# Loading expert weights two experts at a time, with a shorter program around it, in a mixture-of-experts kernel

## The chip, the cores and the metric

The kernel runs on one core of a Trainium2 chip. The metric is the device time of one execution in microseconds (us). Four runs of the kernel before took 181.02 to 181.21 us, with a median of 181.1 us. The profile of the kernel before is one more execution, of 181.01 us.

The engines by the names that the profile uses: PE is TensorE (matrix products), PEld its weight loads, DVE is VectorE, ACT is ScalarE, POOL is GpSimd, SP is SyncE. A trailing q (SPq, PEq) means the engine's sequencer. DMA transfers are issued by SP and POOL here and carried out by 16 DMA engines.

## What is computed

```python
def setup_inputs():
    n_experts, capacity, hidden, expert_hidden = 8, 256, 512, 2048
    # x (8, 256, 512), w1 (8, 512, 2048), w2 (8, 2048, 512), all float32

def reference(x, w1, w2):
    h = np.matmul(x, w1)
    h = np.maximum(h, 0)
    return np.matmul(h, w2).astype(np.float32)
```

Each of eight experts has its own two-layer network and its own 256 rows. The weights are 8.39 MB for one expert in fp32, 67.1 MB in all; x and the output are 4.19 MB each.

## The kernel before

All inputs come from HBM as fp32 and are used as bf16. POOL's DMAs convert while they load; the part of x that SP loads (`x_head`) arrives as fp32 and is converted by DVE.

**Storage.** `w1_sb` and `w2_sb` have `NS` = 4 slots each, and expert e uses slot e mod 4. x has no place of its own: it waits in slot 2 of `w2_sb` (`x_sb`) until it has been transposed into `xT`. `hT` holds one expert's hidden values, and `out_sb` the whole output in fp32.

**The order of work on each engine** is written out by hand inside one critical section (`tc.tile_critical`, line 101), with semaphores between the engines. Each engine enters it after SP has given a signal (SP's no-op of line 101).

- SP issues `x_head` (line 105), then waits for one weight load after another, in the order of `loads`, and tells PE of each through the counters `c_w1` and `c_w2` (lines 109 and 111). At the end it stores the last expert (line 113).
- POOL issues the rest of x (line 119), makes the identity matrix with an affine select (line 122; DVE has set the tile to zero before), and then issues all weight loads (line 154): w1 and w2 of experts 0 to 6, then w1 of expert 7 and its w2 in two halves, 17 loads. Before a load into a slot that was used, it waits until PE is through with the old content: the first layer of expert e - 4 for w1, the second layer for w2. The w2 load of expert 2 waits for the transposes, since x lies in that slot. Before the last half of w2, a tiny store of 3 KB is issued (line 146), and after it the store of experts 0 to 6 (line 157), which waits for expert 6's results and for the tiny store to land.
- PE transposes x (64 matmuls), and then does for each expert: take one count of `c_w1`; the first layer in two halves of 32 matmuls each; the second layer, 32 matmuls, taking a count of `c_w2` ahead of each half. All matmuls stand in the profile under the helper's line 243, and are told apart by what they write: `xt_ps`, `h_ps` (first layer), `o_ps` (second layer). Addresses are kept in registers; `set_expert` works out the next expert's, with the slot from a mod and a multiplication.
- ACT copies half of the transposed x, applies the Relu to the first layer's results (`h_ps` to `hT`, line 202), copies the last piece of the output (line 208), and waits for the two stores to land (lines 209 and 210).
- DVE clears the identity tile (line 172), converts `x_head` (line 176), copies the other half of the transposed x, and copies `o_ps` to `out_sb` (line 185).

Of the kernel before, what the change touches and what calls it, by code (L numbers as in the profile page):

```python
# [8 lines left out]
FP32 = mybir.dt.float32  # L9
BF16 = mybir.dt.bfloat16  # L10
PE = mybir.EngineType.PE

FIRST_FREE = 16512


@with_exitstack
def kernel(
# [7 lines left out]
    nc = tc.nc  # L25
    P = 128
# [30 lines left out]
    def allot(name, shape, dtype):  # L57
        nonlocal free
        places[name] = free
        t = nc.alloc_sbuf_tensor_at(name, shape, dtype, offset=free)  # L60
        free += math.prod(shape[1:]) * mybir.dt.size(dtype)
        return t
# [3 lines left out]
    xT = allot("xT", [P, K1, MC, E * P], BF16)  # L66
    hT = allot("hT", [P, K2, C], BF16)
    out_sb = allot("out_sb", [P, E, MC, H], FP32)
    x_head = allot("x_head", [P, HEAD * H], FP32)
    identity = allot("identity", [P, P], BF16)  # L70
    W1_AT, W2_AT, XT_AT = places["w1_sb"], places["w2_sb"], places["xT"]

# [7 lines left out]
    def sem(name):  # L80
        return tc.alloc_semaphore(name)


    d_head, d_x = sem("d_head"), sem("d_x")
    d_first, d_out, d_last = sem("d_first"), sem("d_out"), sem("d_last")

    s_zero, s_ident, s_cast = sem("s_zero"), sem("s_ident"), sem("s_cast")
    p_xt, p_h, p_o = sem("p_xt"), sem("p_h"), sem("p_o")
    v_out, v_last = sem("v_out"), sem("v_last")

# [1 line left out]
    c_h, c_o, c_w1, c_w2 = sem("c_h"), sem("c_o"), sem("c_w1"), sem("c_w2")  # L92


    loads = []
    for e in range(E - 1):
        loads += [(1, e, 0, 2), (2, e, 0, 2)]
    loads += [(1, E - 1, 0, 2), (2, E - 1, 0, 1), (2, E - 1, 1, 1)]
    d_w = [sem(f"d_w{i}") for i in range(len(loads))]

    with tc.tile_critical(no_gpsimd_drain=True):  # L101


        sp = nc.sync
        sp.dma_start(x_head[:], x_v[:, :HEAD * H]).then_inc(d_head, 16)
        for i, (w, e, h, n) in enumerate(loads):
            sp.wait_ge(d_w[i], 16)
            if w == 1:
                sp.sem_inc(c_w1, 1)
            else:  # L110
                sp.sem_inc(c_w2, n)
        sp.wait_ge(v_last, MC)
        sp.dma_start(
            out_v[:, E - 1, :], out_sb[:, E - 1].rearrange("p m h -> p (m h)")
# [1 line left out]


        pool = nc.gpsimd
        pool.dma_start(x_sb[:, HEAD * H:], x_v[:, HEAD * H:]).then_inc(d_x, 16)  # L119
        pool.wait_ge(s_zero, 1)  # L120

        pool.affine_select(  # L122
            out=identity[:],
# [4 lines left out]
            pattern=[[-1, P]],  # L128
            channel_multiplier=1,
        ).then_inc(s_ident)  # L130
        for i, (w, e, h, n) in enumerate(loads):


            old = e - NS
            if (w, e) == (2, 2):
                pool.wait_ge(p_xt, K1 * MC)
            if old >= 0 and h == 0:
                if w == 1:
                    pool.wait_ge(p_h, NG * (old + 1))
                else:  # L140
                    pool.wait_ge(p_o, MC * (old + 1))
            if i == len(loads) - 1:


                pool.wait_ge(v_out, 1)
                pool.dma_start(  # L146
                    out_v[:16, 0:5:2, :16], out_sb[:16, 0:5:2, 0, :16]
                ).then_inc(d_first, 16)
            if w == 2:
                src = w2_v[:, e, h:h + n, :].rearrange("p h n -> p (h n)")  # L150
                dst = w2_sb[:, e % NS, h * JH * H:(h + n) * JH * H]
            else:
                src, dst = w1_v[:, e, :], w1_sb[:, e % NS, :]
            pool.dma_start(dst, src).then_inc(d_w[i], 16)  # L154
        pool.wait_ge(v_out, 2)
        pool.wait_ge(d_first, 16)
        pool.dma_start(  # L157
            out_v[:, :E - 1, :], out_sb[:, :E - 1].rearrange("p e m h -> p e (m h)")
        ).then_inc(d_out, 16)
        pool.drain()  # L160

# [5 lines left out]


        dve = nc.vector
        dve.memset(identity[:], 0.0).then_inc(s_zero)  # L172
        dve.sem_inc(c_xt[0], 1)
        dve.sem_inc(c_o, MC)
        dve.wait_ge(d_head, 16)
        dve.tensor_copy(x_sb[:, :HEAD * H], x_head[:]).then_inc(s_cast)  # L176
        for ko in range(K1):
            dve.wait_ge(p_xt, ko * MC + 1)
            copy_xt(dve.tensor_copy, ko, 0).then_inc(c_xt[0])
# [10 lines left out]

        act = nc.scalar
        act.sem_inc(c_xt[1], 1)
        act.sem_inc(c_h, UG)
        for ko in range(K1):
            act.wait_ge(p_xt, ko * MC + 2)
            copy_xt(act.copy, ko, 1).then_inc(c_xt[1])
# [9 lines left out]
                ).then_inc(c_h)  # L206
        act.wait_ge(p_o, E * MC)
        act.copy(out_sb[:, E - 1, 1, :], o_ps[1][:]).then_inc(v_last)  # L208
        act.wait_ge(d_out, 16)
        act.wait_ge(d_last, 16)  # L210

# [31 lines left out]
        def loop(name, counter, times, body):  # L245
# [6 lines left out]

        reg = {
            n: pe.alloc_register(n)
            for n in ["count", "half", "slot", "x", "b1", "b2"]
            + [f"xt{ko}" for ko in range(K1)]
            + [f"a{i}" for i in range(12)]
        }
# [2 lines left out]
        def last_column(step):  # L261

            return (P - 1) * step * 2

        count = reg["count"]

        n = MC * (R // MC)

        def transposes():
            i = 0  # L270
            for m in range(MC):
                take(c_xt[m], 1)
                for r2 in range(R // MC):
                    if i % 6 == 0:
                        for k in range(i, min(i + 6, n)):
                            row = (k % (R // MC)) * MC + k // (R // MC)
                            pe.reg_add(bank[i // 6 % 2][k - i], reg["x"], row * H * 2)
                        if i + 6 > n:
                            pe.reg_add(reg["x"], reg["x"], 2)
                            pe.reg_add(count, count, 1)  # L280
                    t = matmul(
                        xt_ps[m][:, r2, :],
                        at(w2_sb, bank[i // 6 % 2][i % 6], [[K1, P]]),
                        pe.lower_ap(identity[:]),
                        start_tensor_calc=True,
                        stop_tensor_calc=True,
                        is_transpose=True,
                    )
                    i += 1
                t.then_inc(p_xt)  # L290

        pe.wait_ge(s_ident, 1)
        pe.wait_ge(s_cast, 1)
        pe.wait_ge(d_x, 16)
        pe.reg_mov(count, 0)
        pe.reg_mov(reg["x"], X_AT + last_column(K1))
        loop("transposes", count, K1, transposes)
        for m in range(MC):
            pe.wait_ge(c_xt[m], 1)

# [30 lines left out]
        def first_addresses():  # L331
            a, b, regs = CHUNKS1[0]
            compute(address1, range(a, b), regs)

        def set_expert():
            slot = reg["slot"]
            pe.reg_mod(slot, count, NS)
            pe.reg_mul(slot, slot, K1 * F * 2)
            pe.reg_add(reg["b1"], slot, W1_AT + last_column(K2))
            pe.reg_add(reg["b2"], slot, W2_AT)  # L340
            for ko in range(K1):
                pe.reg_add(reg[f"xt{ko}"], reg[f"xt{ko}"], P * 2)
            first_addresses()

        def half():
            n = JH * K1
            for i in range(n):
                j, ko = divmod(i, K1)
                c, r = place(CHUNKS1, i)
                if i == CHUNKS1[c][1] - 2:  # L350
                    if c + 1 < len(CHUNKS1):
                        next_chunk(CHUNKS1, c, address1)
                        if c + 2 == len(CHUNKS1):
                            pe.reg_add(reg["half"], reg["half"], 1)
                    else:
                        pe.reg_add(reg["b1"], reg["b1"], JH * 2)
                        first_addresses()
                        a, b, regs = CHUNKS2[0]
                        compute(address2, range(a, b), regs)
                g = j // GJ  # L360
                ends = j % GJ == GJ - 1 and ko == K1 - 1
                if ends:


                    take(c_h, 1)
                    if i == n - 1:
                        take(c_o, MC // 2)
                mm = matmul(
                    h_ps[g][:, (j % GJ) * C:(j % GJ + 1) * C],
                    at(w1_sb, r, [[K2, P]]),  # L370
                    at(xT, reg[f"xt{ko}"], [[E * P, MC], [1, P]]),
                    start_tensor_calc=ko == 0,
                    stop_tensor_calc=ko == K1 - 1,
                )
                if ends:
                    mm.then_inc(p_h)

        def expert():
            take(c_w1, 1)
            loop("half", reg["half"], 2, half)  # L380
            for k in range(K2):
                if k % JH == 0:
                    take(c_w2, 1)
# [4 lines left out]
                if k == CHUNKS2[c][1] - 1 and c + 1 < len(CHUNKS2):  # L388
                    next_chunk(CHUNKS2, c, address2)
                if k == CHUNKS2[-1][0] - 1:  # L390
                    pe.reg_add(count, count, 1)
                    pe.reg_add(reg["half"], reg["half"], -2)
                if k == K2 - 1:
                    set_expert()
                for m in range(MC):
# [7 lines left out]
                    if k == K2 - 1:  # L403
                        mm.then_inc(p_o)

        pe.reg_mov(count, 0)
        pe.reg_add(reg["half"], count, 0)
        pe.reg_add(reg["b1"], count, W1_AT + last_column(K2))
        pe.reg_add(reg["b2"], count, W2_AT)
        for ko in range(K1):  # L410
            pe.reg_add(reg[f"xt{ko}"], count, XT_AT + ko * MC * E * P * 2)
        first_addresses()
        take(c_h, 1)
        loop("expert", count, E, expert)


# [28 lines left out]
```

## Time and profile before

| What | Value |
|---|---|
| Median of four runs | 181.1 us |
| Profiled execution | 181.01 us |
| Its span, first to last instruction | 179.2 us |
| PE busy in the span | 131.0 us |
| ACT busy in the span | 38.7 us |
| Read from HBM, written to HBM | 71.30 MB, 4.20 MB |
| Mean of both over the span | 421 GB/s |
| Start of the first weight load's issue on POOL | 2.45 us |
| Landing of the first weight load (SP's line 109) | 22.6 us |
| Landing of the last weight load (SP's line 111) | 167.9 us |
| First matmul of the first layer | 25.18 us |
| Last store issued on SP (line 113) | 174.80 us |
| Landing of that store, after its issue | 3.1 us |
| Landing of the large store (line 157), after its issue at 163.85 us | 12.8 us |

How to read it: the span counts from the first instruction of the program to the last. The difference between the execution's time and the span, 1.8 us, lies outside what the profile shows of the program. A line of the timeline gives start, duration, engine, source line, operation, output and inputs, the number of instructions merged, and in brackets the idle time of the engine before it and what ended that. A line of the waits gives who waited for whom, the total, how often, and the longest. The page's slices cut the span into 40 equal parts and give a busy share in tenths; in the row PEclk it is the granted TensorE clock.

### The profile page before, as it was taken

Reading aid. Unit: us, or ns where it says so; the run is one execution under the profiler, and the core shown is the slowest. Engines: PE = TensorE matmul, PEld = TensorE weight load, DVE = VectorE, ACT = ScalarE, POOL = GpSimd, SP = SyncE. Lnnn points to the kernel's source line nnn. Section 1 sums busy time; section 2 is a strip of 40 time slices with the busy share of each in tenths; the row PEclk is TensorE's granted clock in tenths of the full one; section 3 lists DMA queues with packets and bytes.
Section 4 is the critical chain, followed back from the end, with each engine's and each line's share of the span. In section 5 each row is a group of like instructions: output and inputs, shape, how many; then the busy total and the mean of one; then the engine's idle time right before and its main releaser. Section 6 shows DMA issues by size and latency. Waiting matters only on the chain. (4 is left out here: it accounts for less than half of the span.)

```text
span 179.2 us, 2111 instructions
## 1 busy us (share of the span) xinstructions
PE 131.0 (73%) x832; PEld 91.6 (51%) x832; DVE 15.9 (9%) x21; ACT 38.7 (22%) x38; POOL 11.7 (7%) x25
## 2 busy tenths in 40 slices
PE   0008659998949494949987698949494998769980
PEld 0007548846924393417933595439341893359530
DVE  0204320002000200020002000020002000200010
ACT  2002423601520044001520044004400152004310
POOL 7100030101010101010011000020000000002000
PEclk9999999999999999996999889999999699978996
DMA  5999999998998999999899899999989989999995
GB/s 194 260 197 227 234 197 212 234 227 183 234 234 186 223 234 197 212 234 227 186 230 234 186 223 234 201 208 234 227 183 234 234 183 227 234 188 222 334 422 239
DMA packets 3824, 40.37 MB, mean 225 GB/s; under 512 B 368, under 2 KB 368, under 8 KB 1392
## 3 DMA queue, kind: packets, MB, share of 16 engines
q0 software_dynamic: 3536, 38.80, 97.1%
q1 hardware_dynamic: 288, 1.57, 2.4%
HBM read 71.30 MB, written 4.20 MB: 421 GB/s over the span
## 5 line engine op out<-in xcount | busy, mean ns | idle before, releaser
L243 PE MATMUL h_ps<-xT,w_sb 128*128 x512 | 67.1, 297 | 18.3 <-PEq L218 18.3
L243 PEld LDWEIGHTS h_ps<-xT,w_sb 128*128 x512 | 60.6, 148 | 26.6 <-issue 22.7
L243 PE MATMUL o_ps<-w_sb,hT 128*128 x256 | 56.5, 379 | 9.2 <-PEq L218 9.2
L202 ACT ACTIVATE hT<-h_ps 128x1024 bf16<-128x1024 f32 x32 | 32.7, 1023 | 111.2 <-PE h_ps L243 111.2
L243 PEld LDWEIGHTS o_ps<-w_sb,hT 128*128 128x128 bf16 x256 | 24.5, 98 | 39.0 <-issue 10.4
L185 DVE COPY out_sb<-o_ps 128x512 f32<-128x512 f32 x15 | 9.7, 686 | 141.2 <-PE o_ps L243 141.2
L243 PE MATMUL xt_ps<-identity,w_sb 128*128 128x128 bf16 x64 | 7.6, 311 | 15.7 <-PEq L218 15.7
L243 PEld LDWEIGHTS xt_ps<-identity,w_sb 128*128 x64 | 6.5, 146 | 16.5 <-issue 16.5
L154 POOL DMA_DIRECT2D w_sb<-in_w_dram x17 | 9.1, 540 | 87.5 <-PE h_ps L243 37.7
L165 ACT COPY xT<-xt_ps 128x1024 bf16<-128x1024 bf16 x4 | 4.0, 1012 | 18.0 <-PE xt_ps L243 18.0
L165 DVE COPY xT<-xt_ps 128x1024 bf16<-128x1024 bf16 x4 | 4.9, 1224 | 11.9 <-PE xt_ps L243 11.9
L157 POOL DMA_DIRECT2D out_dram<-out_sb x1 | 0.9, 947 | 44.3 <-DMA out_dram<-out_sb 44.3
L208 ACT COPY out_sb<-o_ps 128x512 f32<-128x512 f32 x1 | 0.6, 585 | 5.9 <-PE o_ps L243 5.9
L146 POOL DMA_DIRECT2D out_dram<-out_sb x1 | 0.6, 557 | 20.0 <-DVEq L188 20.0
L176 DVE CAST w_sb<-x_head 128x2048 bf16<-128x2048 f32 x1 | 1.2, 1226 | 4.5 <-DMA x_head<-in_x_dram 4.5
L165 ACT ACT_TABLE_LOAD x1 | 1.3, 1283 | 1.0 <-SPq L101 1.0
L119 POOL DMA_DIRECT2D w_sb<-in_x_dram x1 | 0.7, 679 | 1.0 <-DVE identity L172 1.0
L122 POOL TENSOR_SCALAR_AFFINE_SELECT identity<-identity 128x128 bf16<-128x128 bf16 x1 | 0.3, 304 | 0.1
L172 DVE MEMSET identity<- 128x64 uint32 x1 | 0.1, 112 | 1.0 <-SPq L101 1.0
L429 POOL MEMSET const-float32-0.0<- 128x1 f32 x1 | 0.1, 98 | 0.2 <-issue 0.2
L429 POOL MEMSET const-bfloat16-1.0<- 128x1 bf16 x1 | 0.1, 101 | 0.0
L429 POOL MEMSET const-uint8-127<- 128x1 uint8 x1 | 0.1, 101 | 0.0
(1 smaller groups left out, 0.1 us busy)
## 6 DMA issues: line engine op xcount, KB each, us to landing
w_sb<-in_w_dram POOLq DMA_DIRECT2D x15, 2048.0 KB, 65.3
out_dram<-out_sb POOLq DMA_DIRECT2D x1, 3584.0 KB, 12.8
w_sb<-in_w_dram POOLq DMA_DIRECT2D x2, 1024.0 KB, 57.0
w_sb<-in_x_dram POOLq DMA_DIRECT2D x1, 1536.0 KB, 11.4
x_head<-in_x_dram SPq DMA_DIRECT2D x1, 1024.0 KB, 4.7
out_dram<-out_sb SPq DMA_DIRECT2D x1, 512.0 KB, 3.1
out_dram<-out_sb POOLq DMA_DIRECT2D x1, 3.0 KB, 44.8
```

Of the source, the lines that this page charges most:

```text
L119: pool.dma_start(x_sb[:, HEAD * H:], x_v[:, HEAD * H:]).then_inc(d_x, 16)
L122: pool.affine_select(out=identity[:], in_=identity[:], compare_op=mybir.AluOpType.not_equal, fill=1.0, base=0, pattern=[[-1, P]], channel_ ...
L146: pool.dma_start(out_v[:16, 0:5:2, :16], out_sb[:16, 0:5:2, 0, :16]).then_inc(d_first, 16)
L154: pool.dma_start(dst, src).then_inc(d_w[i], 16)
L157: pool.dma_start(out_v[:, :E - 1, :], out_sb[:, :E - 1].rearrange("p e m h -> p e (m h)")).then_inc(d_out, 16)
L165: return copy(xT[:, ko, m].rearrange("k (ep r2) -> k ep r2", r2=R // MC), xt_ps[m][:].rearrange("k r2 ep -> k ep r2"),)
L176: dve.tensor_copy(x_sb[:, :HEAD * H], x_head[:]).then_inc(s_cast)
L185: cp = dve.tensor_copy(out_sb[:, e, m, :], o_ps[m][:])
L202: act.activation(hT[:, g * GJ:(g + 1) * GJ, :].rearrange("p a c -> p (a c)"), h_ps[g % UG][:], mybir.ActivationFunctionType.Relu,).then_in ...
L208: act.copy(out_sb[:, E - 1, 1, :], o_ps[1][:]).then_inc(v_last)
L243: return pe.add_instruction(inst)
L429: nc = _bacc.Bacc("TRN2", target_bir_lowering=False, num_devices=1)
```

## The change

The weight loads are regrouped. w1 of experts (0, 1), (2, 3) and (4, 5), and w2 of experts (0, 1) and (2, 3), are each loaded by one DMA into two neighbouring slots; the rest stays one load an expert, and the last w2 two halves. 17 loads become 12. A pair is announced to PE when both experts have landed. POOL's wait for free slots goes by the later expert of a pair.

With that come other edits:

- `x_head` is a tile of a pool now, and its load and conversion stand ahead of the critical section. All engines but POOL wait for the conversion when they enter it. POOL enters at once and waits for it just before the load of w2 for experts 2 and 3 (`tc.wait_critical_data_deps()`).
- POOL sets the identity tile to zero itself.
- Each slot has one semaphore for its landings, counted up, in place of one semaphore for each load; several others are merged into `d_pool` and `s_ident`.
- PE's expert loop has no counter of its own: the slot's address is stepped and wrapped (`next_slot`), the loop ends on the address of `xT`, and it jumps back to the head of the half loop. The count of `c_w1` is taken in each half, and SP adds two for each expert.
- POOL's drain and ACT's last waits stand behind PE's loop.
- The tiles' addresses move by 8,192 bytes per partition.

```diff
-FIRST_FREE = 16512
+FIRST_FREE = 16512 + 8192
...
     loads = []
-    for e in range(E - 1):
-        loads += [(1, e, 0, 2), (2, e, 0, 2)]
-    loads += [(1, E - 1, 0, 2), (2, E - 1, 0, 1), (2, E - 1, 1, 1)]
-    d_w = [sem(f"d_w{i}") for i in range(len(loads))]
+    for es in [(0, 1), (2, 3)]:
+        loads += [(1, es, 0, 2), (2, es, 0, 2)]
+    loads += [(1, (4, 5), 0, 2), (2, (4,), 0, 2), (2, (5,), 0, 2)]
+    for e in range(6, E - 1):
+        loads += [(1, (e,), 0, 2), (2, (e,), 0, 2)]
+    loads += [(1, (E - 1,), 0, 2), (2, (E - 1,), 0, 1), (2, (E - 1,), 1, 1)]
+    landed, counts = [], {}
+    for w, es, h, _ in loads:
+        s = d_half if h else (d_w1, d_w2)[w - 1][es[0] % NS]
+        counts[id(s)] = counts.get(id(s), 0) + 16
+        landed.append((s, counts[id(s)]))
+
+    x_pool = ctx.enter_context(tc.tile_pool(name="x_pool", bufs=1))
+    x_head = x_pool.tile([P, HEAD * H], FP32, tag="x_head")
+    nc.sync.dma_start(x_head[:], x_v[:, :HEAD * H])
+    nc.vector.tensor_copy(x_sb[:, :HEAD * H], x_head[:])
     with tc.tile_critical(no_gpsimd_drain=True):
 
         sp = nc.sync
-        sp.dma_start(x_head[:], x_v[:, :HEAD * H]).then_inc(d_head, 16)
-        for i, (w, e, h, n) in enumerate(loads):
-            sp.wait_ge(d_w[i], 16)
-            if w == 1:
-                sp.sem_inc(c_w1, 1)
-            else:
-                sp.sem_inc(c_w2, n)
+        for i, (w, es, h, n) in enumerate(loads):
+            sp.wait_ge(*landed[i])
+            sp.sem_inc((c_w1, c_w2)[w - 1], n * len(es))
...
-        pool.wait_ge(s_zero, 1)
+        pool.memset(identity[:], 0.0).then_inc(s_ident)
+        pool.wait_ge(s_ident, 1)
...
-            old = e - NS
-            if (w, e) == (2, 2):
+            old = es[-1] - NS
+            if w == 2 and 2 in es:
+                tc.wait_critical_data_deps()
                 pool.wait_ge(p_xt, K1 * MC)
...
+            e, ne, at_slot = es[0], len(es), es[0] % NS
             if w == 2:
-                src = w2_v[:, e, h:h + n, :].rearrange("p h n -> p (h n)")
-                dst = w2_sb[:, e % NS, h * JH * H:(h + n) * JH * H]
+                src = w2_v[:, e:e + ne, h:h + n, :].rearrange("p e h n -> p e (h n)")
+                dst = w2_sb[:, at_slot:at_slot + ne, h * JH * H:(h + n) * JH * H]
             else:
-                src, dst = w1_v[:, e, :], w1_sb[:, e % NS, :]
-            pool.dma_start(dst, src).then_inc(d_w[i], 16)
+                src, dst = w1_v[:, e:e + ne, :], w1_sb[:, at_slot:at_slot + ne, :]
+            pool.dma_start(dst, src).then_inc(landed[i][0], 16)
         pool.wait_ge(v_out, 2)
-        pool.wait_ge(d_first, 16)
+        pool.wait_ge(d_pool, 32)
...
-        act.wait_ge(d_out, 16)
-        act.wait_ge(d_last, 16)
...
+        def next_slot():
+
+            size, wrap = K1 * F * 2, reg["wrap"]
+            pe.reg_add(wrap, slot, -(NS - 2) * size)
+            pe.reg_alu(wrap, wrap, 0, mybir.AluOpType.max)
+            pe.reg_mul(wrap, wrap, NS)
+
         def set_expert():
-            slot = reg["slot"]
-            pe.reg_mod(slot, count, NS)
-            pe.reg_mul(slot, slot, K1 * F * 2)
+            pe.reg_add(slot, slot, K1 * F * 2)
+            pe.reg_sub(slot, slot, reg["wrap"])
...
         def half():
             n = JH * K1
+            take(c_w1, 1)
...
-        def expert():
-            take(c_w1, 1)
-            loop("half", reg["half"], 2, half)
+        def second_layer():
...
-        loop("expert", count, E, expert)
+        loop("half", reg["half"], 2, half)
+        second_layer()
+        pe.br_lt(reg["xt0"], xt_first[0] + E * P * 2, on_true="half_head", on_false="experts_end")
+        nc.switch_bb("experts_end")
+
+
+        pool.drain()
+        act.wait_ge(d_pool, 48)
+        act.wait_ge(d_last, 16).then_inc(s_ident)
```

## The prediction

> **What bounds the kernel now.** First the page: busy shares, the slices, the queues.
>
> ```profile
> span 179.2 us, 2111 instructions
> PE 131.0 (73%) x832; PEld 91.6 (51%) x832; DVE 15.9 (9%) x21; ACT 38.7 (22%) x38; POOL 11.7 (7%) x25
> PEclk9999999999999999996999889999999699978996
> DMA  5999999998998999999899899999989989999995
> q0 software_dynamic: 3536, 38.80, 97.1%
> ```
>
> TensorE is busy for 73% and the DMA engines are full in all slices but the first and last. Is the stream dense, or does it wait for anything? SP passes each landed weight load on, so its waits and the times of its two lines (109 for w1, 111 for w2) show the pace of the stream:
>
> ```profile
> SPq L109 <- DMA w_sb<-in_w_dram: 88.8, 8, 21.2
> SPq L111 <- DMA w_sb<-in_w_dram: 77.2, 9, 9.7
> ...
> L109 SPq EVENT_SEMAPHORE  x8: 17/17/17, 22.6 to 158.2; - x8
> ```
>
> (158.2 - 22.6) / 7 = 19.37 us an expert, for 8.39 MB of fp32 read: 433 GB/s. The landings of the trace are even: 22.58, 32.25, 41.95, 51.62 ... 148.49, 158.18, 163.04 and 167.93 us. No load was issued late: the median one was issued 65 us before it landed. Then the end, in the timeline:
>
> ```profile
> 155.55 1.29 DVE L185 COPY out_sb<-o_ps 128x512 f32<-128x512 f32 x2 [18.09 <-PE o_ps L243]
> 158.35 8.85 PE L243 MATMUL h_ps<-xT,w_sb 128*128 x64 [2.62 <-PEq L218]
> ...
> 163.85 0.95 POOL L157 DMA_DIRECT2D out_dram<-out_sb  x1 [44.30 <-DMA out_dram<-out_sb]
> ...
> 167.09 7.07 PE L243 MATMUL o_ps<-w_sb,hT 128*128 x32
> ...
> 174.19 0.58 ACT L208 COPY out_sb<-o_ps 128x512 f32<-128x512 f32 x1 [5.93 <-PE o_ps L243]
> 174.80 0.35 SPq L113 DMA_DIRECT2D out_dram<-out_sb  x1
> ```
>
> The page's chain (PE, then ACT) stops at the last computation, but the kernel does not: the store of experts 0 to 6 moves packets from 167.19 to 176.28 us, directly behind the last weights, and the last expert's store from 175.90 to 177.53. So the DMA engines have work without a pause from 1.96 us (first packet of x_head) to 177.53 us. Some 1.7 us of barriers follow. That is the bound: when the first byte moves, how densely the rest follows, and what is left behind the last one. TensorE waits 2.6 us before each expert.
>
> **The change part by part.**
>
> Start. SP's x_head load at line 105 starts at 0.95 us. Before it stand SP's signal to the critical section (line 101, at 0.73) and its wait for that signal (0.80). Afterwards the load stands ahead of both. It can gain nothing, or at most 0.95 - 0.73 = 0.22 us; I take 0.15, since its own setup stays. POOL no longer waits for SP's signal, so x's other load is issued no later; its packets started at 4.83 us only, when x_head's were nearly through. The price is that DVE, ACT, PE and SP now wait for the cast of x_head to enter the section, at about 6.9 us. Behind that wait stand ACT's table load (1.28 us; ACT's first copy is at 15.4), PE's transposes (they wait for x until 12.9 anyway) and SP's first landing (32 us). All covered. POOL's new memset, at most the 0.30 us of the affine select on the same tile, delays the first weight load from 2.45 us to about 3; x keeps the engines until 12.5. The no-op at line 149 holds POOL until the cast; the load behind it waits for the transposes (23.6 us) in any case.
>
> Five fewer loads. 17 become 12, with the same bytes. What does the boundary between loads cost? 2 MB take 9.686 us (148.493 to 158.179), a 1 MB half 4.865: 2 x 4.865 - 9.686 = 0.044 us per boundary. Five are worth 0.22 us if the cost is per load. The halves also have twice as many packets for their bytes, so it may lie in the packets, and then a pair gains nothing. The completion packet alone took 22 ns, half of the 44: I take 0.15. The other end: a pair's source has two rows per partition, 4 MB apart, which no row shows. Nearest is x's load, which takes 24 KB out of every 32 KB: 12,288-byte packets in 926 ns against 16,384 in 1,226 ns, so 26.5 against 26.7 B/ns read, 0.7% less. On 5 pairs x 19.37 us that loses 0.7 us.
>
> [...]
>
> When weights come. Without other shifts the pairs land at 32.25 (w1 of 0, 1), 51.62 (w2), 71.0 (w1 of 2, 3), 90.38 (w2), 109.74 (w1 of 4, 5); the rest as before. TensorE, with 7.38 us a first layer and 7.07 a second at full clock, and 1.7 more where it starts cold (the 3.4 us dips of the granted clock to 0.5 make 8.85 to 8.99 of 7.38): first layer of 0 at 32.4 to 41.3, wait; second layer at 51.8 to 60.6; expert 1 to 75.0; first layer of 2 to 82.4, wait 8 us; second at 90.5 to 99.3; then experts 3 to 6 without a wait, 4 x 14.45 = 57.8, to 157.1. Every load is there by then: w2 of 4 at 119.43 is wanted at 121, w2 of 5 at 129.11 wanted at 135, w2 of 6 at 148.49 wanted at 150. The delay is made good 1 us before w1 of 7 lands (158.18). The last expert then starts as now, and needs the last half of w2 (167.93) in any case.
>
> POOL's waits for free slots. w1 of (4, 5) now needs the first layer of expert 1 (75.0 - 7.07 = 67.9), with w2 of (2, 3) in the queue until 90.4; w2 of 4 and of 5 need 60.6 and 75.0; w1 of 6 needs 82.4; w2 of 6 needs 99.3, with work queued until 138.8; w1 and w2 of 7 need 106.7 and 113.7. The tiny store and the last half need expert 4's copies, about 128 + 1.6, and the half starts at 163. No gap; the least cover is 22 us, and beyond that delay each microsecond would lengthen the kernel by one.
>
> Tail. The big store still waits for the tiny one, which lands with the first half of w2. If TensorE is warm in the last expert it ends at 172.5 instead of 174.15, and the last store is issued 1.5 us earlier. But the engines are full: 1,024 output packets at 51 per 0.5 us take 10.04 us from 167.19, until 177.23 against 177.53. Gain 0 (cold) to 0.3; I take 0.1.
>
> Teardown. ACT takes one branch fewer behind the last wait (33 ns and its gap), and some 13 fewer semaphores stand in the range clear of 0.27 us: 0 to 0.2, I take 0.1. Register arithmetic on PE (no mod, three more operations) lies under matmuls until 90 us and then inside TensorE's 1 us of slack.
>
> Sum: -0.15 - 0.15 - 0.1 - 0.1 = -0.5 us. The profiled execution took 181.01 us, 179.2 of it span; 1.8 lies outside, unchanged. So 178.7 span and 180.5; its run stood 0.1 under the median of 181.1, so 180.6.
>
> **The rivals.**
>
> *Nothing arrives* (181.1): the boundary cost is in the packets, x_head's first bytes wait for something other than SP, and the tail is cold. For it: each term is a tenth or two, and none has a row of its own. Against: lines 101 and 105 stand in series.
>
> *The pairs read more slowly* (slower). Place: the five paired loads, 97 us of stream. Price: 0.7 us at x's pace, so 180.6 + 0.15 + 0.7 = 181.45; 1% is 1.0 us, 181.7. It outweighs the other gains (0.35) from 0.36% on. For it: the engines already run at 433 GB/s without slack, so any loss shows fully. Against: neither x's odd rows nor the change between w1 and w2 shows more than 0.7%.
>
> *TensorE becomes the bound* (slower). From 90.5 us it runs behind. With a cold start in each expert, 15.9 us instead of 14.45, it ends at 90.5 + 8.8 + 5 x 15.9 = 178.8, 4.6 late: 185. It decides from 15.0 us an expert (74.9 us left for five). The return from a second to a first layer is never seen without a DMA wait; the tightest, 41.45 to 42.12, allows at most 0.67 us, 15.1 an expert. Against: the dips follow idle stretches of 2.6 us, and there are none here.
>
> *More than I count* (180.0): the pairs' packets are larger, or fewer instructions shorten the 1.8 us outside the span.
>
> **How the numbers follow.** Forecast 0.54, nothing 0.22, slower reading 0.12, TensorE 0.06, more 0.06. The forecast's own range is 180.2 (all bounds: -0.22 - 0.22 - 0.3 - 0.2 = -0.94) to 181.0. The range of 180.0 to 181.6 takes in "nothing" and the near half of slower reading. The measurement tells 0.2%, 0.36 us, from no change. Faster, under 180.74: four fifths of the forecast and all of "more", 0.50. Same: a fifth of the forecast, "nothing", 0.32. Slower, over 181.46: 0.18.
>
> **What would show it.** Right: x_head issued near 0.8 us; paired landings 19.32 to 19.37 us apart; the last half landing near 167.6; PE without a wait from 90 to 156 us; last packet near 177.1. Wrong: paired landings over 19.5 us apart, a gap in the stream before w1 of 4 and 5, or the last expert's first layer starting after 159 us.

## The result: slower by a quarter of a per cent

The changed kernel takes 181.58 us (median of 46 runs, 181.27 to 182.49), the kernel before 181.13 us (70 runs beside it, 180.92 to 181.98). The ratio is 1.0025, with a 95% interval of 1.0019 to 1.0031. The profiled execution of the changed kernel took 181.40 us. The time lies inside the range that was given, but on the wrong side of no change: a gain of 0.5 us was forecast, and 0.45 us were lost.

The page of the changed kernel, with the rows that answer to those shown of before (the queues are the last three of them):

```profile
span 179.6 us, 2102 instructions
PE 128.0 (71%) x832; PEld 89.9 (50%) x832; DVE 15.8 (9%) x20; ACT 38.7 (22%) x38; POOL 10.3 (6%) x21
...
PEclk9999999999558999999558999999999999999998
DMA  6998999999899999999999999998999999899994
...
q0 software_dynamic: 3456, 38.80, 96.8%
q1 hardware_dynamic: 288, 1.57, 2.4%
q8 instruction: 1, 0.02, 0.0%
```

The page of before has two queues:

```profile
q0 software_dynamic: 3536, 38.80, 97.1%
q1 hardware_dynamic: 288, 1.57, 2.4%
```

The span is 0.4 us longer. POOL's queue (q0), which carries the weights, moves the same 38.80 MB in 3,456 packets, 80 fewer than before. The last row of the changed kernel is new: one transfer of instructions, 0.02 MB, on a queue of its own. It looks like nothing, at 0.0% of 16 engines' span. It turned out to be the difference between forecast and result. Below, "the transfer" means this one.

The start of `x_head` in the timeline of before, and then the start and the end in that of the changed kernel:

```profile
0.95 0.38 SPq L105 DMA_DIRECT2D x_head<-in_x_dram  x1
```

```profile
0.74 0.38 SPq L116 DMA_DIRECT2D x_head<-in_x_dram  x1
...
1.91 0.22 POOL L132 MEMSET identity<- 128x128 bf16 x1
...
2.81 2.18 POOL L169 DMA_DIRECT2D w_sb<-in_w_dram  x3 [0.15 <-issue]
...
74.42 7.51 PE L252 MATMUL h_ps<-xT,w_sb 128*128 x64
...
91.12 9.24 PE L252 MATMUL o_ps<-w_sb,hT 128*128 x31 [9.19 <-PEq L227]
...
158.92 7.49 PE L252 MATMUL h_ps<-xT,w_sb 128*128 x64 [1.32 <-PEq L227]
...
164.36 0.97 POOL L172 DMA_DIRECT2D out_dram<-out_sb  x1 [32.71 <-DMA out_dram<-out_sb]
...
166.31 7.07 PE L252 MATMUL o_ps<-w_sb,hT 128*128 x32
...
174.02 0.35 SPq L125 DMA_DIRECT2D out_dram<-out_sb  x1
```

x_head is issued 0.21 us earlier than before, as forecast. POOL's new memset takes 0.22 us, and the first weight load is issued at 2.81 us (forecast about 3). TensorE begins the last expert 0.57 us later than before (158.92 against 158.35), because its w1 landed at 158.75 instead of 158.18, but runs it at the full clock (7.49 us instead of 8.85), and the last store is issued at 174.02 instead of 174.80 us. The large store (line 172), which waits for a landing, is issued 0.51 us late. And the last store needs longer now. This is its row among the DMA issues of the page (KB, and us from issue to landing), and behind it the DMA engines' mean busy tenths from 176 to 179 us, 0.075 us a digit, first of before and then, with the GB/s, of the changed kernel:

```profile
out_dram<-out_sb SPq DMA_DIRECT2D x1, 512.0 KB, 4.5
```

```profile
DMA  9899979997979979561000000000000000000000
```

```profile
DMA  5969999997949170201010101010000000000000
GB/s 218 601 273 437 437 382 492 382 437 328 546 164 492 55 273 0 109 0 55 0 55 0 55 0 55 0 55 0 0 0 0 0 0 0 0 0 0 0 0 0
```

The store lands 4.5 us after its issue, at 178.47 us (before: 3.1, at 177.90). From about 177.3 us the row reads 0 and 1 by turns: 55 GB/s for 0.075 us is one packet of 4 KB, every second slice. I read this as a single DMA engine still at work; by the trace the last store's 15th completion of 16 came at 177.73 us, the 16th at 178.47.

Where does it fall behind? The trace has 16 completions for each load, which I take as one from each of the 16 engines. A load has landed with the last of them. The landings, and the distance between the first and the last of the 16, from the trace:

```
load            w1 (0,1)  w2 (0,1)  w1 (2,3)  w2 (2,3)  w1 (4,5)  ...  last half  last store
landing, us       32.12     51.48     70.87     90.95    110.31        168.51      178.47
first to 16th      0.49      0.49      0.53      1.26      1.27          1.30        1.27
```

The steps are 19.36, 19.39, 20.08 and 19.36 us. One step is 0.7 us too long, the engines are 0.73 us further apart after it, and stay so to the end. Inside that step lies the instruction transfer: one packet of 16,384 bytes, from 75.03 us on, 0.945 us long. The queues in the window from 73 to 78 us:

```profile
q0 software_dynamic: 63, 1.03, 96.9%
q8 instruction: 1, 0.02, 1.2%
```

The packets show it directly. A weight packet starts as the transfer ends, at 75.96 us, and takes 1.416 us, where nearly all 1,920 of its size take 1.227. It is the longest of them, and so is the packet behind the transfer in each of the nine profiles below that have one (1.395 to 1.418 us). Its 0.19 us more and the transfer's 0.945 are 1.13 us on one engine. The landings move by less because this engine need not have been the last one before.

The distance stays at 1.25 to 1.30 us at all later landings: I read this as the late engine not catching up, which fits queues whose packets took 99.2% of 16 engines' span (96.8 and 2.4). In this run, what one engine lost at 75 us was still missing at the end.

### The profile page after: what moved, and what is told of

Its sections match the earlier page's. It is cut to its first block, busy times and chain, and to the rows that moved or that the text cites. A ratio compares the mean times of both kernels' runs of the same rounds, so it can differ in the third digit from the quotient of the medians.

```text
span 179.6 us, 2102 instructions
## 1 busy us (share of the span) xinstructions
PE 128.0 (71%) x832; PEld 89.9 (50%) x832; DVE 15.8 (9%) x20; ACT 38.7 (22%) x38; POOL 10.3 (6%) x21
## 2 busy tenths in 40 slices
DMA packets 3745, 40.39 MB, mean 225 GB/s; under 512 B 288, under 2 KB 288, under 8 KB 1312
## 3 DMA queue, kind: packets, MB, share of 16 engines
q0 software_dynamic: 3456, 38.80, 96.8%
## 5 line engine op out<-in xcount | busy, mean ns | idle before, releaser
L252 PE MATMUL o_ps<-w_sb,hT 128*128 x256 | 60.6, 398 | 18.6 <-PEq L227 18.6
L252 PE MATMUL h_ps<-xT,w_sb 128*128 x512 | 61.5, 281 | 11.2 <-PEq L227 10.5
L252 PEld LDWEIGHTS h_ps<-xT,w_sb 128*128 x512 | 57.9, 146 | 15.7 <-issue 13.1
L252 PEld LDWEIGHTS o_ps<-w_sb,hT 128*128 128x128 bf16 x256 | 25.4, 101 | 51.0 <-issue 24.5
L169 POOL DMA_DIRECT2D w_sb<-in_w_dram x12 | 7.4, 618 | 106.2 <-PE h_ps L252 57.4
```

Source lines behind the costliest of these rows:

```text
L169: pool.dma_start(dst, src).then_inc(landed[i][0], 16)
L252: return pe.add_instruction(inst)
```

## The experiments

Fifteen kernels were run beside the kernel before. Where a kernel has one run, its time is that of the profiled execution, and no interval goes with it. "Length" is the number of instructions of TensorE in the compiled program, and the last column is the start of the instruction transfer in the kernel's own profile, which is one execution.

| Kernel | TensorE's loop, length | us (runs) | ratio to before | transfer at, us |
|---|---|---|---|---|
| before | old, 214 | 181.13 (70) | | none |
| changed | new, 210 | 181.58 (46) | 1.0025 [1.0019, 1.0031] | 75.03 |
| unpaired | new, 210 | 181.56 (10) | 1.0021 [1.0005, 1.0036] | 59.48 |
| before_paired | old, 214 | 181.08 (10) | 0.9987 [0.9970, 1.0004] | none |
| pe_214 | new, 214 | 181.50 (10) | 1.0018 [1.0006, 1.0030] | 112.54 |
| dve_pool_pads | new, 210 | 181.37 (1) | | 73.78 |
| after_old_pe | old, 214 | 180.62 (6) | 0.9968 [0.9956, 0.9981] | none |
| before_new_pe | new, 209 | 181.13 (10) | 1.0001 [0.9992, 1.0011] | none |
| pe_226 | new, 226 | 181.43 (1) | | 60.56 |
| pe_tail_222 | new, 222 | 181.59 (1) | | 75.23 |
| old_pe_unpaired | old, 214 | 180.81 (9) | 0.9983 [0.9973, 0.9993] | none |
| new_pe_plus1 | new, 210 | 182.13 (1) | | 61.01 |
| new_pe_plus16 | new, 225 | 181.93 (1) | | 40.21 |
| old_pe_plus16 | old, 230 | 181.53 (1) | | 59.44 |
| pe_209 | new, 209 | 180.66 (11) | 0.9980 [0.9969, 0.9992] | none |
| old_pe_plus1 | old, 215 | 180.87 (1) | | none |
| old_pe_plus6 | old, 220 | 180.88 (1) | | none |

**Is it the pairs?** `unpaired` is the changed kernel with 17 single loads:

```diff
-    for es in [(0, 1), (2, 3)]:
-        loads += [(1, es, 0, 2), (2, es, 0, 2)]
-    loads += [(1, (4, 5), 0, 2), (2, (4,), 0, 2), (2, (5,), 0, 2)]
-    for e in range(6, E - 1):
+    for e in range(E - 1):
         loads += [(1, (e,), 0, 2), (2, (e,), 0, 2)]
```

> The changed kernel with one load an expert again (17 loads). In the changed kernel's trace one transfer of 16,384 B of instructions starts at 75.03 us, takes 0.945 us, and from the next landing on the slowest of the 16 DMA engines is 0.75 us further behind (spread 0.53 us at 70.9, 1.26 us at 91.0 and ever after). Theory A, the fetch costs the time and comes from the edits around the loads (the shorter TensorE program, 210 instructions instead of 214): the fetch stays, and the time is 181.4 to 181.7. Theory B, the pairs cost it (by slower reading, or because the fetch comes with them): the landings' spread stays under 0.55 us to the end, and the time is 180.6 to 180.9.

It is as slow as the changed kernel, 181.56 us, and its page has the same row:

```profile
span 179.9 us, 2104 instructions
...
q8 instruction: 1, 0.02, 0.0%
```

So the loss is not in the pairs. With single loads the transfer comes at 59.48 us, and the engines' distance goes from 0.64 to 1.23 us at the next landing. The last half of w2 lands at 168.73 us, 0.8 later than before; 0.2 of that was there ahead of the transfer (51.83 against 51.62 us).

`before_paired` puts the pairs alone into the kernel before (the list of loads and POOL's addresses as in the change, and SP's counts):

```diff
-                sp.sem_inc(c_w1, 1)
+                sp.sem_inc(c_w1, len(es))
             else:
-                sp.sem_inc(c_w2, n)
+                sp.sem_inc(c_w2, n * len(es))
```

> The kernel before with the pairs alone. Theory A: no instruction fetch in the span, five paired loads 19.35 us apart instead of 19.37, last half landing about 0.1 us earlier than 167.93, 180.9 to 181.1. Theory B: a fetch or slower pairs, 181.5 to 181.9.

It took 181.08 us, and the interval takes in no change. There is no transfer. Its profiled execution (181.47 us) was a long one for this kernel, with pairs 19.43 to 19.59 us apart: 256 of its 1,920 weight packets took over 1.24 us, against 6 in the profile before. In the profiles of `after_old_pe`, `pe_209` and `old_pe_plus6` below, which have pairs too, none does, and the pairs are 19.32 to 19.39 us apart. So it isn't the pairs that make packets slow, and this one execution tells little. What made its packets slow is open.

**Which engine's instructions?** The changed kernel has fewer instructions on TensorE. `pe_214` brings TensorE's program back to the length of before:

```diff
+        s_pad = sem("s_pad")
+        for _ in range(4):
+            pe.sem_inc(s_pad, 1)
         pe.wait_ge(s_ident, 2)
```

> The changed kernel with four more TensorE instructions (increments of a semaphore that nobody reads) ahead of the transposes, 214 as in the kernel before. Theory A in the form that the length of TensorE's program decides whether a fetch falls into the span: no 16 KB fetch, landings' spread under 0.55 us throughout, 180.6 to 180.9. If the fetch belongs to another engine or to the pairs: fetch near 75 us as now, 181.4 to 181.7.

The transfer only moved, to 112.54 us, and the kernel takes 181.50 us. The length as such doesn't decide. `dve_pool_pads` gives POOL and DVE two such instructions each:

```diff
+        s_pad = [sem(f"s_pad{i}") for i in range(2)]
+        for _ in range(2):
+            pool.sem_inc(s_pad[1], 1)
...
+        for _ in range(2):
+            dve.sem_inc(s_pad[0], 1)
```

> The changed kernel with two more instructions on POOL ahead of its weight loads and two more on DVE ahead of its first copy. At 75.03 us POOL had just issued w2 of expert 5 (74.89), DVE was starting the second copy of expert 1 (75.02), and TensorE had just jumped back to the first layer for the second time (74.2). If POOL's place in its program sets off the fetch, it moves to about 68 us; if DVE's, to about 61 us; if TensorE's, it stays near 75.0 us. In each case the time stays at 181.3 to 181.8.

The transfer stays within 1.3 us of its place (73.78 against 75.03), so what DVE and POOL execute has little to do with it.

**TensorE's program by itself.** `after_old_pe` is the changed kernel with the TensorE program of before: its counter, its mod, its loop over experts. SP's count for w1 goes with it:

```diff
-            sp.sem_inc((c_w1, c_w2)[w - 1], n * len(es))
+            sp.sem_inc((c_w1, c_w2)[w - 1], (1 if w == 1 else n) * len(es))
...
-        loop("half", reg["half"], 2, half)
-        second_layer()
-        pe.br_lt(reg["xt0"], xt_first[0] + E * P * 2, on_true="half_head", on_false="experts_end")
-        nc.switch_bb("experts_end")
+        loop("expert", count, E, expert)
```

> The changed kernel with TensorE's program of the kernel before (expert loop with a counter, first-layer loop nested in it, slot from a mod), pairs and all other edits as changed. Theory C: the new loop, which jumps from the second layer straight back into the head of the first layer's loop, sets off the 16 KB instruction fetch (in each of the four traces with it, the fetch starts 3.2 to 4.3 us after a jump back of 211 ns instead of 201, whichever iteration that is). Then there is no fetch here, the landings' spread stays under 0.55 us, and the time is 180.6 to 180.9, under both kernels. Theory D, another engine's program or chance: fetch in the span, 181.4 to 181.7.

180.62 us: faster than both kernels, ratio 0.9968 [0.9956, 0.9981]. There is no transfer in its page (3,744 packets where the changed kernel has 3,745), and the last expert starts as before:

```profile
span 178.8 us, 2104 instructions
...
DMA packets 3744, 40.37 MB, mean 226 GB/s; under 512 B 288, under 2 KB 288, under 8 KB 1312
```

```profile
158.12 9.00 PE L252 MATMUL h_ps<-xT,w_sb 128*128 x64 [2.62 <-PEq L227]
```

The pairs land at 32.11, 51.46, 70.81, 90.16 and 109.52 us: 19.35 to 19.36 apart, all four steps. `before_new_pe` is the other half, the new TensorE program in the kernel before (the registers and loops of the change, and the counts that go with them):

```diff
-                sp.sem_inc(c_w1, 1)
+                sp.sem_inc(c_w1, 2)
...
-        act.sem_inc(c_h, UG)
+        act.sem_inc(c_h, UG - 1)
...
-        loop("expert", count, E, expert)
+        loop("half", reg["half"], 2, half)
+        second_layer()
+        pe.br_lt(reg["xt0"], xt_first[0] + E * P * 2, on_true="half_head", on_false="experts_end")
+        nc.switch_bb("experts_end")
```

> The kernel before with TensorE's program of the changed one alone (209 instructions), loads one by one. Theory C: a 16 KB fetch in the span, one DMA engine 0.7 to 0.9 us behind from then on, 181.7 to 182.0. Theory D: no fetch, 181.0 to 181.2.

181.13 us, ratio 1.0001, no transfer. So the new loop is not slow in itself: here, one instruction shorter, it runs without a transfer. Two more look at how the length acts. `pe_226` is `pe_214` with `range(16)`; `pe_tail_222` has 12 such instructions behind the loop, so that nothing in front of it moves:

```diff
         nc.switch_bb("experts_end")
+        for _ in range(12):
+            pe.sem_inc(s_pad, 1)
```

> The changed kernel with 16 more TensorE instructions ahead of the transposes (226), which move the loop's place in the program. If the loop's place decides, the fetch goes away or falls before the span's loads: spread under 0.55 us, 180.6 to 180.9. If the loop's shape decides, the fetch stays: 181.3 to 181.8.

> The changed kernel with 12 more TensorE instructions behind the loop (222): the loop stays where it is and only the program's end moves. If the end of the program decides whether more is fetched, the fetch goes away: 180.6 to 180.9. If the loop's shape or place decides, the fetch stays: 181.3 to 181.8.

With the pads behind the loop the transfer stays where it was (75.23 against 75.03 us); with pads ahead of it, it moves to 60.56. In these two kernels, each run once, what counted was where the loop lay in the program (or the transposes' loop, which the pads ahead move with it), not how long the program was.

**What the rest is worth.** `old_pe_unpaired` has the old TensorE program (the diff of `after_old_pe`) and single loads (the diff of `unpaired`), so only the edits at the start and the end are left of the change:

> The changed kernel with TensorE's old program and with one load an expert: the edits at the start and the end alone. Against the same kernel with pairs (180.62, no fetch). If the boundary between loads is worth 0.02 to 0.044 us each (five of them), as the even landings say, 180.7 to 180.85; if the pairs gain nothing, 180.55 to 180.7. First landing 0.1 to 0.2 us before 22.58 in either case, no fetch.

180.81 us, 0.9983 [0.9973, 0.9993]. So start and end are worth some 0.3 us. From here to `after_old_pe` it is another 0.19 by the medians, but the two intervals overlap, and `before_paired` is not clear of no change either: the times alone don't show a gain of the pairs. The landings do, and a smaller one. From the landing of x to that of the fifth pair `after_old_pe`, `pe_209`, `old_pe_plus1` and `old_pe_plus6` take 96.76 us each; with single loads the kernel before, `before_new_pe` and `old_pe_unpaired` take 96.85 to 96.86 to the same weights. That is 0.1 us for five loads (the long execution of `before_paired`, 97.42, is left aside).

**Does one instruction bring the transfer, and into any program?** `new_pe_plus1` and `new_pe_plus16` are `before_new_pe` with `range(1)` and `range(16)` in the diff of `pe_214`; `old_pe_plus16` is `after_old_pe` with `range(16)` there.

> The kernel before with TensorE's new program and one more instruction ahead of the transposes: 210 instructions, and the loop starts where it starts in the changed kernel, one further than in the run without a fetch. If the loop's place in TensorE's program decides by itself, a 16 KB fetch appears and one DMA engine falls 0.7 to 0.9 us behind: 181.7 to 182.0. If the other engines' edits are needed too, no fetch: 181.0 to 181.3.

> The same with 16 more instructions (225). The changed kernel has the fetch at each place of the loop that was tried (0, 4 and 16 further). If the place decides, fetch and 181.7 to 182.0; if the other engines' edits decide, no fetch and 181.0 to 181.3.

> The changed kernel with TensorE's old program and 16 instructions more ahead of the transposes (230): does the old loop keep free of the fetch when it is moved? If the loop's shape protects it: no fetch, 180.55 to 180.8. If only its place did: fetch, 181.3 to 181.6.

All three have the transfer, and all three are slow: 182.13, 181.93 and 181.53 us. With one pad (209 to 210) the engines' distance goes from 0.41 to 1.87 us at one landing, and is 1.06 to 1.20 at all later ones. (Its 182.13 us are not all the transfer's: 122 of its weight packets took over 1.24 us, which adds some 0.3 us to each engine's share.) The old loop gets it too, if it lies 16 instructions further on. So neither loop is the cause by its form.

**The cure with the smallest edit.** `pe_209` is the complete change, pairs and new loop, with TensorE's wait for the identity matrix moved to DVE, which gives TensorE its first signal:

```diff
+        dve.wait_ge(s_ident, 2)
         dve.sem_inc(c_xt[0], 1)
...
-        pe.wait_ge(s_ident, 2)
```

> The changed kernel, complete, with one TensorE instruction fewer: DVE waits for the identity tile before it gives TensorE the first count for the transposes, so TensorE's own wait for it goes (209 instructions, the loop's head one place earlier, where the run without a fetch had it). If the loop's place decides: no fetch, landings' spread under 0.55 us to the end, 180.55 to 180.75, faster than the kernel before by 0.2 to 0.35%. If something else in the changed kernel calls the fetch: fetch in the span, 181.4 to 181.7.

180.66 us, 0.9980 [0.9969, 0.9992]; the transfer is gone from its page, and its end, 176 to 179 us in the same view as above, has no tail of single packets:

```profile
span 178.9 us, 2101 instructions
...
q0 software_dynamic: 3456, 38.80, 97.2%
q1 hardware_dynamic: 288, 1.57, 2.4%
```

```profile
DMA  9999999797969141100000000000000000000000
```

The row reads 0 from 177.3 us on; no single engine is left behind. Landings are 32.10, 51.45, 70.84, 90.16, 109.51 ... 167.76, and the last store 177.70, with 0.32 to 0.47 us between first and 16th. One instruction taken off TensorE is worth 181.58 - 180.66 = 0.92 us by the medians.

`old_pe_plus1` and `old_pe_plus6`, with `range(1)` and `range(6)`, looked for the edge of the old loop between 214 and 230:

> The changed kernel with TensorE's old program and one more instruction (215). If the old program stands at an edge as the new one does at 209: fetch, 181.3 to 181.6. If it has room: no fetch, 180.55 to 180.8.

> The same with six more instructions (220). With 0 there was no fetch, with 16 there was. Fetch: 181.3 to 181.6; none: 180.55 to 180.8.

Neither has the transfer. With 180.87 and 180.88 us in one run each they lie a little over what was expected. So the edge lies above 220.

**What stays open** is why the place of the loop decides. In each profile with the transfer TensorE jumped back to a loop's head 2.4 to 4.3 us earlier, and that jump took 211 to 221 ns where most take 201 to 203 (the first one of the transposes' loop takes 220 to 228 ns with or without a transfer). In the changed kernel it is the jump at 70.73 us. The one at 56.40 us took as long, and no transfer followed it. They are the longest of the outer loop (ns, shortest, median and longest):

```profile
L432 PEldq COMPARE_BRANCH  x8: 69/201/211, 56.4 to 169.4; - x8
```

But profiles without the transfer have such a jump as well (`pe_209` at 56.97, `old_pe_plus6` 221 ns at 56.73), so it is a companion and not shown as the cause. Why the transfer comes at one iteration and not at another was not settled either. That the program fetched is TensorE's is inferred from what brings and removes it; the trace does not name its owner.

## Why the prediction was wrong in direction

**The bound: right, and more strictly than it was used.** The stream of transfers shows no slack to speak of: the packets of q0 and q1 took 99.5% of 16 engines' span before (97.1 and 2.4), and 0.945 us on one engine cost the changed kernel some 0.9 us. The prediction used that against the loads ("any loss shows fully") and asked only whether the weights themselves would be read more slowly. It did not ask what else uses the DMA engines.

**The step that failed** is the cost of TensorE's new program: "Register arithmetic on PE (no mod, three more operations) lies under matmuls until 90 us and then inside TensorE's 1 us of slack." For the arithmetic that holds. From 91.12 to 157.6 us TensorE computes without a wait, 66.5 us where 90.5 to 157.1 was worked out. What was missed is a transfer of instructions that takes a DMA engine's time from the weights (the next weight packet started at 75.96 us, as it ended); the sum had nothing for it. At 75.03 us TensorE is in a first layer that runs through (74.42 us, 64 matmuls, 7.51 us, where `pe_209`, without the transfer, took 7.46): the transfer cost TensorE next to nothing, and cost the stream 0.945 us of one engine, 1.13 with the slow packet behind it. By pairs of kernels that differ in TensorE's program, it is worth 0.92 us (changed and `pe_209`), 0.96 (changed and `after_old_pe`, 180.62) and 0.75 (`unpaired` and `old_pe_unpaired`). With 0.9 us put into the forecast's sum, -0.5 becomes +0.4; measured was +0.45.

**Without the transfer the sum of the forecast stands**: 180.62 and 180.66 us against 180.6. Its terms came out less well, so that part of the agreement is luck. In the profiles of `old_pe_unpaired`, `after_old_pe` and `pe_209`, each one execution, they are:

- Start, forecast -0.15: x_head is issued 0.21 us earlier in the changed kernel, the first pair lands 0.13 earlier there (32.12 against 32.25), the first load 0.07 earlier in `old_pe_unpaired` (22.51 against 22.58). Of that nothing is left at the last half with single loads (167.92 against 167.93). By the medians, start, tail and teardown together are worth 0.35 us (181.16 for the kernel before beside it, 180.81), of which the teardown shows 0.17. So the start brings between 0 and 0.2; the runs don't fix it more closely.
- Five fewer loads, -0.15: 0.1 us over the paired stretch (96.76 us against 96.85), so 0.02 per boundary. The 0.19 of the medians is not clear of noise, and the 0.20 by the last half of w2 (167.92 to 167.72) holds 0.06 of an earlier start (x landed at 12.82 and 12.76 us). 0.02 us is what the completion packet took (22 ns), and half of the 0.044 that the 1 MB halves gave. The larger bound of 0.22 didn't come.
- Tail, -0.1: nothing to be seen. In the changed kernel and in `old_pe_unpaired` the last store was issued at 174.02 and 173.31 us, and landed no earlier for it: without the transfer 177.87 against 177.90. As the prediction said, the engines are full then: from 167.2 to 177.5 us before, 38 of 40 slices of the DMA row read 9.
- Teardown, -0.1: from the last landing to the end of the span 1.33 us before, 1.16 after, -0.17. The 1.8 us outside the span are unchanged (181.40 - 179.63 = 1.77), so the fourth rival's second reason falls.

**The rivals.** "The pairs read more slowly" fell: steps of 19.32 to 19.39 us in the clean profiles against 19.37 before, so that the second rows, 4 MB off, cost nothing that the steps show. The rival had put the outcome on the right side of zero and at nearly the right time (181.45), for a reason that doesn't hold. That 181.58 lies inside the range is luck for the same cause: its upper end of 181.6 was set for this rival. Its sign, paired landings more than 19.5 us apart, even occurred: once in the changed kernel (20.08), through the transfer, and three times in the long execution of `before_paired` (19.51 to 19.59), without one. A long step in the landings tells that an engine was late, not why. "TensorE becomes the bound" fell with the 1.3 us wait before expert 7, 2.0 to 2.6 without the transfer. "Nothing arrives" fell with the kernels without the transfer (0.9968 and 0.9980, both intervals below 1).

## What to carry to other kernels

If a kernel is bound by a DMA stream without a pause, look in the page's list of queues for an instruction queue, in the kernel before and after, whatever the edit was meant to do: a row of 0.0% cost 0.9 us here. TensorE's program here is short through its loops, 210 instructions, and had the transfer all the same, while 209 ran without it; one instruction moved to another engine was enough to take it away, and which number of instructions is safe had to be tried. Compare the first and the last of the 16 completions of each load: where they spread and stay apart, as from 0.53 to 1.26 us here, one engine may have been given other work, and the moment of the spread says where to look.

## What the runs showed of the hardware that was not expected

- One transfer of 16,384 bytes kept its engine for 0.945 us, less than the 1.227 us of a weight packet, which writes as many bytes and reads twice as many; but the weight packet behind it took 1.395 to 1.418 us in all nine profiles. In these nine profiles the distance between the engines grew by 0.6 to 1.0 us (in `new_pe_plus1` by 1.5 at first, by 0.8 at the next landing), and until the last half of w2 no more than some 0.2 of it was taken back.
- With the new loop, 209 instructions on TensorE ran without the transfer and 210 had it, in the kernel before (`before_new_pe`, `new_pe_plus1`) as in the changed one (`pe_209`, changed). With the old loop 214, 215 and 220 ran without and 230 had it.
- The granted clock of TensorE fell for longer than in the profile before. There, while TensorE had work left, it has four dips of 3.41 us, from 80.82, 101.30, 138.84 and 159.32 us: at the end of waits of 2.61 to 2.62 us or some 1 us behind it (two more such waits, until 61.48 and 119.60 us, show none). In the changed kernel two dips three times as long begin inside waits of 9.43 and 9.19 us that the pairs bring; the wait of 9.20 us before expert 0 shows none. Four neighbouring windows of the changed kernel (behind the window's length PE's busy time; third from the right the granted clock):

```profile
44.80:48.20 3.40, 0.00 (x0) 0.00 (x0) 0.00 (x0) 0.00 (x0) 0.00 (x0) 0.50 0.95 202
48.20:51.60 3.40, 0.00 (x0) 0.00 (x0) 0.00 (x0) 0.00 (x0) 0.00 (x0) 0.50 1.09 231
51.60:55.00 3.40, 3.36 (x8) 1.20 (x9) 0.00 (x0) 0.00 (x0) 0.00 (x0) 0.50 1.08 231
55.10:58.50 3.40, 3.40 (x18) 1.51 (x17) 0.00 (x0) 0.00 (x0) 0.00 (x0) 1.00 1.08 231
```

The trace has the clock at 0.5 from 44.79 to 55.03 us and again from 85.75 to 95.99, 10.24 us each time. It cost TensorE 1.7 us in the second layer of expert 0 (8.72 us instead of 7.07), which the wait of 9.19 us before w2 of 2 takes up.
